# Attention scores with the keys on the partitions: one change to a two-layer hybrid block

## The chip, the cores and the metric

The kernel runs on one core of a Trainium2 chip. A core has a matrix engine (TensorE, PE in the profile; its weight loads are PEld), a vector engine (VectorE, DVE), ScalarE (ACT), GpSimd (POOL) and a queue for transfers (SyncE, SP). Each executes its own instructions in program order and waits for the others by semaphores. The metric is the device time of one execution in microseconds; lower is better.

## The reference, cut to what matters

Two layers of a block over 1024 latent tokens and 256 context tokens, width 1024. Each layer normalizes and modulates, multiplies by one input projection, and splits its columns among a bidirectional gated DeltaNet (a recurrence over chunks of tokens), a latent attention with four heads, and a short convolution. All are gated, concatenated and sent through one output projection. Only the attention is touched here:

```python
def mla_queries(q_a, norm_g, w_qb, cos, sin):
    q = (rmsnorm(q_a, norm_g) @ w_qb).reshape(bn, t, B_HEADS, B_NOPE + B_ROPE)   # 4 heads x (64 + 32)
    if cos is not None:
        q = jnp.concatenate([q[..., :B_NOPE], rope_2d(q[..., B_NOPE:], cos, sin)], axis=-1)
    return q
...
        s = jnp.einsum("bqhd,bkhd->bhqk", q_blk, k).astype(F32) * scale
        p = jax.nn.softmax(s, axis=-1).astype(v.dtype)
        return jnp.einsum("bhqk,bkhd->bqhd", p, v)
...
    b_x = softmax_attention(q_x, jnp.concatenate([k_x, k_c], axis=1),
                            jnp.concatenate([v_x, v_c], axis=1)) * jax.nn.silu(xz_b)
```

Latent queries read all 1280 keys, context queries (first layer only) the 256 context keys. All data are float32.

## The kernel before

Tokens are cut into ten tiles of 128: 0 to 7 are latent, 8 and 9 context. `GROUPS` joins them to pieces of 512, 512 and 256 tokens. A layer is a chain of stages: gate and convolution blocks with the large input projection (L447), preparation of the recurrence's chunks, and then a stage in which the attention and the recurrence run side by side, and at whose end the output projection starts. That stage is where the change lies.

Products that need nearly full precision are made from three passes of a high and a low part (`mm3`, L83): high by high, low by high, high by low. A low part is the value less its high part, which is one DVE instruction, after an ACT copy that rounds to the high part. Products of probabilities and values, of the recurrence, and transposes by the identity matrix are plain float32.

The attention of one layer, before. `k_pair` (L1013 to L1026) makes the keys of two heads, 64 channels from the compressed keys and 32 rotary ones, in `kh` and `kl` (latent, high and low) and `kc` (context). `v_tile` makes the values of a token tile. `q_tile` makes the queries of one token tile: two transposes (L827, L828), six passes of 384 columns with the queries as the stationary operand, the rotation on POOL (L345 to L350), four transposes (L844), and the split into high and low parts (L848). The unit of work is a query tile and a head, 40 in the first layer and 32 in the second:

- `a_scores` (L1031): 128 queries on the partitions, keys as moving columns in pieces of 512, 512 and 256, three passes each; DVE takes the row maximum of each piece (L1041) and of the three (L1045); ACT takes the exponential with the negated maximum as the bias and sums the row as it goes (L1048).
- `a_trans` (L1053): ten transposes of the probabilities (L1058), copied out by ACT and DVE (L1060).
- `a_pv` (L1065): probabilities by values, 64 output channels of one head in one half of the array's columns and of the other head in the other half (`tile_position`, L1074).
- `a_out` (L1085): the reciprocal row sums are transposed, spread over the partitions by a small matmul (L1095), and multiplied with the result and the gate.

The recurrence, `recur` (L1107 to L1189), one generator for each direction, has four kinds of products per tile and direction (L1144, L1154, L1164, L1169 and L1170) and vector instructions between them (L1146, L1156, L1173, L1181; L1150 on POOL).

What sets the order: a small planner, `Sched` (L85), holds generators as lanes with a due time. The attention loop (L1302) writes its instructions directly and calls `sch.tick(dt)` with a guessed duration; each tick advances the planner's clock and lets the lanes that are due issue their next piece. The instruction order of each engine that comes out of this is rearranged once more by the framework's scheduler when the kernel is built, so the order of the code is only roughly that of the engines.

Of the kernel before, what the change touches and what calls it, by code (L numbers as in the profile page):

```python
# [14 lines left out]
KD = 8  # L15
NT = 10
# [5 lines left out]
C_ID, C_SUM, C_UP, C_LO, C_ONE, C_COS, C_SIN, C_SEL, C_END = 0, 128, 160, 288, 416, 544, 672, 800, 1056  # L22
# [6 lines left out]
def kernel(  # L29
# [16 lines left out]
    cst_in: bass.AP,  # L46
    out: bass.AP,
# [95 lines left out]
    bx_d = dram([128, NT, 2, 128], "bx_d")  # L143
# [142 lines left out]
    # the first modulation  # L286
# [28 lines left out]
    for l in range(DEPTH):  # L315
# [4 lines left out]
        # token-layout block  # L320
# [52 lines left out]
        # gates  # L373
# [50 lines left out]
        # channel-layout blocks  # L424
# [126 lines left out]
        # z and short-conv blocks  # L551
# [53 lines left out]
        # chunk preparation  # L605
# [170 lines left out]
        # weights and keys of the latent attention  # L776
# [3 lines left out]
        def load_qkv():  # L780
            wq_r = st([128, 2, 384], "P4", name="wq_r")
            S.dma_start(out=wq_r[:, 0], in_=mla_w_qb[l, 0:128, :])
            S.dma_start(out=wq_r[0:64, 1], in_=mla_w_qb[l, 128:192, :])
# [4 lines left out]
            wq = st([128, 2, 2, 384], "W8", F32R, name="wq")  # L788
            for b_, m in ((0, 128), (1, 64)):
                V.tensor_scalar(wq_r[0:m, b_], wq_r[0:m, b_], col[0:m, 75 + b_:76 + b_], sc, ALU.mult, ALU.mult)  # L790
                split(wq_r[0:m, b_], wq[0:m, 0, b_], wq[0:m, 1, b_])
# [4 lines left out]
            sch.add(q_tile(act[0]))  # L796
# [3 lines left out]
        def kv_lane(i):  # L800
            while len(merged) < NT:
                yield 1.0
            if "c" not in qkv:
                qkv["c"] = [st([128, TOK], "T5", F32R, name=f"ckv{w}") for w in range(2)]
                qkv["pe"] = st([128, TOK], "T5", name="pes")
            ckv, pes = qkv["c"], qkv["pe"]
# [13 lines left out]
        Q = {}  # L820

        def q_tile(i):
            mq = st([128, 192], "P2", name="mq")
            S.dma_start(out=mq, in_=mla_d[i, :, 0:192])
            yield 3.0
            pt = bank()
            T.transpose(pt[:, 0:128], mq[:, 0:128], ident)  # L827
            T.transpose(pt[0:64, 128:256], mq[:, 128:192], ident)  # L828
            qa = st([128, 2, 2, 128], "P2", F32R, name="qa")
            for b_, m in ((0, 128), (1, 64)):  # L830
                src = pt[0:m, b_ * 128:b_ * 128 + 128]
                copy_a(qa[0:m, 0, b_], src)
                V.tensor_tensor(out=qa[0:m, 1, b_], in0=src, in1=qa[0:m, 0, b_].bitcast(F32), op=ALU.subtract)
            yield 2.0
            pq = bank()
            mm3(pq[:, 0:384], [(qa[0:m, a_, b_], qkv["wq"][0:m, w_, b_]) for b_, m in ((0, 128), (1, 64)) for a_, w_ in ((0, 0), (1, 0), (0, 1))])
            qs = st([128, 4, 96], "P2", name="qs")
            copy_a(qs.rearrange("p h f -> p (h f)"), pq[:, 0:384])
            if i < NX:
                rope(qs[:, :, 64:96], i, 4)  # L840
            yield 6.0
            pt = bank()
            for h in range(4):
                T.transpose(pt[0:96, h * 128:(h + 1) * 128], qs[:, h, :], ident)  # L844
            qt = st([128, 2, 4, 128], "P4", F32R, name="qt")
            p3 = pt[0:96].rearrange("p (h f) -> p h f", h=4)
            copy_a(qt[0:96, 0], p3)
            V.tensor_tensor(out=qt[0:96, 1], in0=p3, in1=qt[0:96, 0].bitcast(F32), op=ALU.subtract)  # L848
            Q[i] = dict(qt=qt, sums=st([128, 4, 3], "st", name="sums"), P={}, PT={}, o={})

        # the start of a layer: two gate blocks beside the rows of h that are still being made
# [148 lines left out]
        # latent attention  # L1000
# [3 lines left out]
        vx = st([128, NT, 256], "B16", name="vx")  # L1004
# [7 lines left out]
        def k_pair(h0):  # L1012
            ws = wk[:, :, 64 * h0:64 * h0 + 128]  # L1013
            for g in (2, 0, 1):
# [4 lines left out]
                for r in range(2):  # L1019
# [5 lines left out]
                    copy_a(hi[64:96], pes[64:96, cs])  # L1025
                    (V if h < 2 else P).tensor_tensor(out=lo[64:96], in0=pes[64:96, cs], in1=hi[64:96].bitcast(F32), op=ALU.subtract)  # L1026

        def a_parts(i):
            return [(g, t0, n) for g, (t0, n) in enumerate(GROUPS) if i < NX or g == 2]

        def a_scores(i, h):  # L1031
            q = Q[i]
            qt = q["qt"]
            pr = a_parts(i)
            mx = st([128, 4], "st", name="mx")
            banks = []
            for g, t0, n in pr:
                pb = bank()
                kk = (kh[0:96, h, t0:t0 + n], kl[0:96, h, t0:t0 + n]) if g < 2 else (kc[0:96, 0, h, :], kc[0:96, 1, h, :])
                mm3(pb[:, 0:n], ((qt[0:96, 0, h], kk[0]), (qt[0:96, 1, h], kk[0]), (qt[0:96, 0, h], kk[1])))  # L1040
                V.tensor_reduce(mx[:, g:g + 1], pb[:, 0:n], AX.X, ALU.max)  # L1041
                banks.append(pb)
            g0 = pr[0][0]
            nm = st([128, 1], "st", name="nm")
            V.tensor_reduce(nm, mx[:, g0:3], AX.X, ALU.max, negate=True)  # L1045
            p = st([128, TOK], "T5", name="prob")
            for (g, t0, n), pb in zip(pr, banks):
                A.activation(out=p[:, t0:t0 + n], in_=pb[:, 0:n], func=ACTF.Exp, bias=nm, scale=1.0, accum_out=q["sums"][:, h, g:g + 1])  # L1048
            q["P"][h] = p
# [366 lines left out]
```

## Time and profile before

| quantity | value |
|---|---|
| median of three runs | 1771.2 us (1770.02 to 1771.27) |
| profiled execution, first to last instruction | 1772.6 us |
| mean granted TensorE clock | 0.984 of full speed |
| busy PE / DVE / ACT / POOL | 97% / 62% / 48% / 26% |
| attention stage of the first layer | 552.7 to 833.1 us |
| attention stage of the second layer | 1408.0 to 1672.5 us |
| PE busy in those two | 532.65 of 544.90 us |

The profile gives for each group of instructions its busy time and the mean duration of one. On PE neighbouring matmuls overlap, so the mean duration is longer than what one adds; the distance from one start to the next tells that. A float32 matmul leaves two records, so that counts of records are twice the number of matmuls there (L1074: 1312 records, 656 matmuls).

### The profile page before, as it was taken

The page shows a single profiled execution, that of the slowest core. Times are in us where ns is not written, and L with a number is a line of the kernel's source. Part 1 is how long each engine was busy: PE and PEld are TensorE (multiplying, and loading weights), DVE is VectorE, ACT ScalarE, POOL GpSimd, SP SyncE. Part 2 cuts the span into 40 slices and gives each one's busy share as a digit, 9 for nine tenths or more (in the row PEclk, how much of TensorE's full clock was granted, in tenths as well). Part 3 has the DMA queues.
Part 4 walks back from the last instruction along what each step waited for, and adds up shares of the span by engine and source line. Part 5 has one row for each costly group of instructions (what it writes and reads, how often), then busy time and mean ns, then how long its engine had stood idle before and what let it go on. Part 6 is the DMA issues. An engine that isn't in the chain of part 4 may idle for free.

```text
span 1772.6 us, 33569 instructions
## 1 busy us (share of the span) xinstructions
PE 1717.4 (97%) x12644; PEld 1430.9 (81%) x12644; DVE 1101.7 (62%) x2178; ACT 842.7 (48%) x2287; POOL 467.5 (26%) x779
## 2 busy tenths in 40 slices
PE   7999999999999999999999999998999899999998
PEld 5787887788878989888887987786787689997786
DVE  3435668787634676656566156599885476675564
ACT  4644663223536444665345346551334655445631
POOL 1410435222211212322230302562113211123221
PEclk8999999999999999999999999998999899999999
DMA  9333556563335866323343224556434535553541
GB/s 365 123 109 100 178 169 188 178 202 101 100 123 184 278 200 196 103 69 127 124 125 129 81 71 133 181 166 212 138 116 123 183 122 181 163 180 113 161 131 48
DMA packets 194770, 264.74 MB, mean 149 GB/s; under 512 B 48304, under 2 KB 116912, under 8 KB 194608
## 3 DMA queue, kind: packets, MB, share of 16 engines
q1 hardware_dynamic: 194608, 262.59, 45.9%
q8 instruction: 100, 1.64, 0.4%
q14 instruction: 62, 0.51, 0.1%
HBM read 183.17 MB, written 79.36 MB: 148 GB/s over the span
## 4 chain that ended last, share of the span: by engine, by line
PE 83%; DVE 6%; DMA 5%; ACT 3%; issue 2%; POOL 1%; SPq 1%; POOLq 0%; DVEq 0%; ACTq 0%
PE bank L447 33%; PE bank L83 23%; PE bank L1074 5%; PE bank L1058 5%; PE bank L1154 2%; PE bank L1144 2%; PE bank L1164 2%; PE bank L1170 2%; PE bank L1169 2%; DMA wa<-in_w_ada_dram 1%; PE bank L511 1%; PE bank L187 1%; DVE pr L675 1%; DVE Mb L676 1%; DMA gcb<-row_d 1%
## 5 line engine op out<-in xcount | busy, mean ns | idle before, releaser
L447 PE MATMUL bank<-h_hi,w 128*128 128x512 f32 x1664 | 433.2, 403 | 2.4 <-DVE h_hi L282 2.4
L447 PEld LDWEIGHTS bank<-h_hi,w 128*128 128x128 f32 x1664 | 305.2, 189 | 75.2 <-issue 4.8
L447 PE MATMUL bank<-h_lo,w 128*128 128x512 f32 x832 | 217.5, 402 | 0.0
L447 PEld LDWEIGHTS bank<-h_lo,w 128*128 128x128 f32 x832 | 154.2, 189 | 37.3 <-issue 1.6
L461 DVE SCALAR_TENSOR_TENSOR acc<-pad,col,acc 128x1284 f32<-128x1284 f32 (+1 forms) x104 | 158.0, 1520 | 8.5 <-ACT acc L458 6.8
L83 PE MATMUL bank<-wo_hi,mix 128*128 128x512 f32 x576 | 141.7, 398 | 0.0
L1048 ACT ACTIVATE prob<-bank,nm 128x512 f32<-128x512 f32 (+1 forms) x200 | 119.4, 607 | 28.3 <-DVE nm L1045 28.1
L1041 DVE TENSOR_REDUCE mx<-bank 128x1 f32<-128x512 f32 (+1 forms) x200 | 112.5, 591 | 23.4 <-PE bank L83 22.6
L83 PEld LDWEIGHTS bank<-wo_hi,mix 128*128 128x128 f32 x576 | 106.9, 188 | 24.8
L75 DVE TENSOR_TENSOR w<-wr,w 128x1024 fp32r<-128x1024 f32 x52 | 66.0, 1271 | 85.1 <-ACT w L74 84.8
L447 PE MATMUL bank<-h_c,w 128*128 128x256 f32 x816 | 110.1, 287 | 0.0
L447 PEld LDWEIGHTS bank<-h_c,w 128*128 128x128 f32 x816 | 102.5, 190 | 6.6 <-issue 4.5
L1150 POOL TENSOR_TENSOR ring<-ring,qx 128x512 f32<-128x512 f32 x32 | 40.7, 1272 | 215.6 <-DMA ring<-row_d 126.9
L1058 PE MATMUL bank<-cst,prob 128*128 128x128 f32 x656 | 94.9, 282 | 2.8 <-ACT prob L1048 2.5
L1074 PE MATMUL bank<-probT,vx 128*64 128x128 f32 x1312 | 97.4, 280 | 0.0
L74 ACT ACTIVATE w<-wr 128x1024 fp32r<-128x1024 f32 x52 | 54.9, 1060 | 73.7 <-PE bank L447 54.7
L1074 PEld LDWEIGHTS bank<-probT,vx 128*64 128x64 f32 x1312 | 78.5, 139 | 12.8 <-issue 7.8
L1060 DVE COPY probT<-bank 128x512 f32<-128x512 f32 x64 | 44.3, 692 | 68.1 <-PE bank L1058 65.5
L83 PE MATMUL bank<-kh,qt 96*128 96x512 f32 x256 | 86.1, 417 | 0.5 <-DVE kl L1024 0.4
L1058 PEld LDWEIGHTS bank<-cst,prob 128*128 128x128 f32 x656 | 71.8, 142 | 18.1 <-issue 11.2
L78 ACT ACTIVATE probT<-bank 128x256 f32<-128x256 f32 (+1 forms) x136 | 61.9, 488 | 35.4 <-PE bank L1058 35.3
L676 DVE TENSOR_TENSOR Mb<-Mb,pr 128x31 f32<-128x31 f32 (+15 forms) x186 | 70.4, 378 | 5.0
(298 smaller groups left out, 3329.8 us busy)
## 6 DMA issues: line engine op xcount, KB each, us to landing
wr<-in_w_blk_dram SPq DMA_DIRECT2D x52, 512.0 KB
wa<-in_w_ada_dram SPq DMA_DIRECT2D x32, 512.0 KB
gcb<-row_d SPq DMA_DIRECT2D x20, 512.0 KB
nn_d<-N SPq DMA_DIRECT2D x20, 512.0 KB
ring<-vr_d SPq DMA_DIRECT2D x40, 256.0 KB
ring<-nn_d SPq DMA_DIRECT2D x40, 256.0 KB
ring<-kt_d SPq DMA_DIRECT2D x40, 256.0 KB
qk_d<-gcb SPq DMA_DIRECT2D x18, 512.0 KB
```

Of the source, the lines that this page charges most:

```text
L74: A.activation(out=hi, in_=raw, func=ACTF.Copy)
L75: eng.tensor_tensor(out=lo, in0=raw, in1=hi.bitcast(F32), op=ALU.subtract)
L78: A.activation(out=out, in_=in_, func=ACTF.Copy)
L83: T.matmul(outp, lhsT=lh, rhs=rh, start=q == 0, stop=q == n - 1)
L447: T.matmul(pb[:, 0:n], lhsT=self.w[:, wi, k, :], rhs=hg[g][hi][:, k, :], start=q + k == 0, stop=q == 2 and k == KD - 1)
L461: V.scalar_tensor_tensor(out=acc[:, 2:hi], in0=pad[:, 2 + t - r:hi + t - r], scalar=col[:, ci:ci + 1], in1=acc[:, 2:hi], op0=ALU.mult, op1 ...
L676: V.tensor_tensor(out=N[:, 0:k, k:32], in0=N[:, 0:k, k:32], in1=pv, op=ALU.subtract)
L1041: V.tensor_reduce(mx[:, g:g + 1], pb[:, 0:n], AX.X, ALU.max)
L1048: A.activation(out=p[:, t0:t0 + n], in_=pb[:, 0:n], func=ACTF.Exp, bias=nm, scale=1.0, accum_out=q["sums"][:, h, g:g + 1])
L1058: T.transpose(pT[:, k * 128:(k + 1) * 128], p[:, t0 + k * 128:t0 + (k + 1) * 128], ident)
L1060: V.tensor_copy(out=pb[:, t0:t0 + n], in_=pT[:, 0:n])
L1074: T.matmul(o3[64 * r:64 * r + 64, pair, :], lhsT=vx[:, kt, hh * 64:hh * 64 + 64], rhs=q["PT"][hh][:, kt * 128:(kt + 1) * 128], start=kt == ...
```

## The change

Scores are made the other way round, for a group of queries and a pair of heads at a time: 128 keys on the partitions (the stationary operand), up to 512 queries as moving columns. The probabilities come out with the keys on the partitions, as the product with the values wants them, and that product is 512 columns wide. There are six such units in the first layer and four in the second.

A maximum per query cannot be a bias any more, since the queries now lie along the columns. It is found by a separate pass, `a_max` (queries on the partitions, high parts only, for one query tile and head), one unit ahead; `a_shift` transposes the negated maxima to row 96 of the queries' tile, and the keys have a row of ones there, so that the first of the three passes has 97 rows of contraction and subtracts the maximum. Before the first unit, `warm` issues all eight maxima of it; in the first layer the two small context units are warmed, and the eight maxima of the third unit are issued within the second one's only step.

The row sums are taken by adding the probabilities over key tiles, head 0 of the pair on DVE (L1122) and head 1 on POOL (L1120), and at the end a product with ones (L1132) adds over the partitions; a reciprocal of 128x512 (L1135) follows. The queries are made in channel layout, 512 tokens at a time: `q_rows` transposes the rows of a group (L846, L847), `q_head` makes a head with five passes of 512 columns (the last two stack high and low part of the 64 remaining rows) and rotates with extra weight columns and a table `rot` (L871, L872 on DVE, one sum on POOL). The weights of the output projection are loaded in tiles of 512 columns, and the attention's result goes to memory as [2, 128, tokens].

```diff
-        def a_scores(i, h):
...
-                mm3(pb[:, 0:n], ((qt[0:96, 0, h], kk[0]), (qt[0:96, 1, h], kk[0]), (qt[0:96, 0, h], kk[1])))
-                V.tensor_reduce(mx[:, g:g + 1], pb[:, 0:n], AX.X, ALU.max)
...
-                A.activation(out=p[:, t0:t0 + n], in_=pb[:, 0:n], func=ACTF.Exp, bias=nm, scale=1.0, accum_out=q["sums"][:, h, g:g + 1])
+        def a_max(g, h, j):
...
+                T.matmul(pb[:, 0:n], lhsT=q["qt"][0:96, 0, j * 128:(j + 1) * 128],
+                         rhs=kh[0:96, h, t0:t0 + n] if gk < 2 else kc[0:96, 0, h, :], start=True, stop=True)
+                V.tensor_reduce(mx[:, gk:gk + 1], pb[:, 0:n], AX.X, ALU.max)
+            V.tensor_reduce(q["nm"][:, j:j + 1], mx[:, 2 if g == 2 else 0:3], AX.X, ALU.max, negate=True)
+        def a_shift(g, h):
...
+                T.transpose(pn[0:1, j * 128:(j + 1) * 128], q["nm"][:, j:j + 1], ident)
+            copy_a(q["qt"][96:97, 0, 0:n], pn[0:1, 0:n])
+        def a_scores(u, kts):
...
+            for kk, kt in enumerate(kts):
+                for r in range(2):
...
+                    mm3(pb, [(hi[0:97], qt[0:97, 0, 0:n]), (hi[0:96], qt[0:96, 1, 0:n]), (lo[0:96], qt[0:96, 0, 0:n])])
+                    A.activation(out=pts[r][:, kk, 0:n], in_=pb, func=ACTF.Exp)
+                sch.tick(0.0028 * n)
-        def a_trans(i, h):
...
+        def a_pv(u, kts, pts):
...
+                    T.matmul(u["po"][64 * r:64 * r + 64, 0:n], lhsT=vx[:, kt, hh * 64:hh * 64 + 64], rhs=pts[r][:, kk, 0:n],
+                             start=kt == keys[0], stop=kt == keys[-1], tile_position=(0, 64 * r))
...
+                    if r:
+                        P.tensor_tensor(acc, a0, a1, ALU.add)
+                    else:
+                        V.tensor_tensor(out=acc, in0=a0, in1=a1, op=ALU.add)
+        def a_out(u):
...
+                T.matmul(sm[64 * r:64 * r + 64], lhsT=cst[:, C_ONE:C_ONE + 64], rhs=vt[:, 5 + r, 0:n], start=True, stop=True,
+                         tile_position=(0, 64 * r))
+            V.reciprocal(out=rc, in_=sm)
+            V.tensor_tensor(out=rc, in0=u["po"][:, 0:n], in1=rc, op=ALU.mult)
+            P.tensor_tensor(zb, zb, rc, ALU.mult)
...
+        def q_head(g, h):
...
+            mm3(pq, [(wq[:, 0, h], qa[:, 0, 0:n]), (wq[:, 0, h], qa[:, 1, 0:n]), (wq[:, 1, h], qa[:, 0, 0:n]),
+                     (wq[:, 2, h], qb[:, 0:n]), (wq[:, 3, h], qb[:, 0:n])])
...
+            V.tensor_tensor(out=lo[0:w], in0=pq[0:w], in1=hi[0:w].bitcast(F32), op=ALU.subtract)
+                V.tensor_tensor(out=r1[64:96], in0=pq[64:96], in1=rot[64:96], op=ALU.mult)
+                V.tensor_tensor(out=r2[64:96], in0=pq[96:128], in1=rot[96:128], op=ALU.mult)
...
+        def warm(u, vs):
+            for g, h in heads(u):
+                q_head(g, h)
+            sch.tick(2.4)
+            mg = maxes(u)
+            for i in vs:
+                next(mg, None)
+                v_tile(i)
+                sch.tick(0.9)
...
+            for q, kts in enumerate(steps):
+                pts = a_scores(u, kts)
+                if prev:
+                    a_pv(*prev)
...
+                    many = 8 if len(steps) == 1 else (0, 2, 3, 3, 0)[q]
+                    for _ in range(many):
+                        next(mg)
+                        sch.tick(0.6)
+                    if q == len(steps) - 1:
+                        for gh in heads(nxt):
+                            a_shift(*gh)
```

Below, what this does to the order of the engines at three places. In the changed kernel the lines of the recurrence stand 40 lower (L1144 is L1184, L1154 is L1194, L1164 is L1204) and `mm3` is L84.

First PE, before, in the second layer's attention: transposes of queries (L844) and of probabilities (L1058), recurrence, and PV (L1074, on `probT` and `vx`).

```order
L1164 MATMUL bank<-vd,ring_14513 128x128 x8
L1144 MATMUL bank<-ring_14513,kx 128x128 x5
L844 MATMUL bank<-cst,qs 96x128 x4
L1074 MATMUL bank<-probT,vx 64x128 x9
L1144 MATMUL bank<-ring_14513,kx 128x128 x2
L1074 MATMUL bank<-probT,vx 64x128
L1144 MATMUL bank<-ring_14513,kx 128x128
L1074 MATMUL bank<-probT,vx 64x128 x10
L1058 MATMUL bank<-cst,prob 128x128 x10
L1154 MATMUL bank<-ring_14513,ring_14512 128x128 x4
```

And PE in the changed kernel in the middle of the first layer's attention, where PV is L1109 (on `probT` and `vt`), the pass for the maxima L1072.

```order
L1109 MATMUL bank<-probT,vt 64x512
L1194 MATMUL bank<-ring_5654 128x128 x4
L1072 MATMUL bank<-kh,qt 128x512 x2
L1072 MATMUL bank<-kc,qt 128x256
L1109 MATMUL bank<-probT,vt 64x512
L1072 MATMUL bank<-kh,qt 128x512
L1109 MATMUL bank<-probT,vt 64x512
L1072 MATMUL bank<-kh,qt 128x512
L1109 MATMUL bank<-probT,vt 64x512
L1072 MATMUL bank<-kc,qt 128x256
```

Before, the 20 matmuls of a PV are cut into runs of nine, one and ten by recurrence products; now single ones, one head's each, stand between recurrence products and passes for the maxima.

Next DVE in the changed kernel, first layer, second context unit: L867, L871 and L872 belong to `q_head`, L1074 and L1075 are the maxima, L1213 the recurrence.

```order
L867 TENSOR_TENSOR qt<-bank,qt 64x512
L871 TENSOR_TENSOR r_6163<-bank,rot 32x512
L872 TENSOR_TENSOR r_6164<-bank,rot 32x512
L867 TENSOR_TENSOR qt<-bank,qt 64x512
L871 TENSOR_TENSOR r_6180<-bank,rot 32x512
L872 TENSOR_TENSOR r_6181<-bank,rot 32x512
L1074 TENSOR_REDUCE mx<-bank 128x1 x3
L1075 TENSOR_REDUCE nm<-mx 128x1
L1213 SCALAR_TENSOR_TENSOR ring_5654<-ring_5654,gtot,bank 128x128 x8
L1074 TENSOR_REDUCE mx<-bank 128x1 x3
L1075 TENSOR_REDUCE nm<-mx 128x1
L1074 TENSOR_REDUCE mx<-bank 128x1 x9
```

All 24 reductions of the third unit's maxima stand in one stretch here; before, three reductions followed each unit's scores.

Then PE in the changed kernel at the same place: the last maxima, the transposes that carry them to row 96 (L1082), and the first scores of the unit.

```order
L1072 MATMUL bank<-kh,qt 128x512 x2
L1072 MATMUL bank<-kc,qt 128x256
L1072 MATMUL bank<-kh,qt 128x512 x2
L1072 MATMUL bank<-kc,qt 128x256
L1082 MATMUL bank<-cst,nm 1x128 x8
L84 MATMUL bank<-qt,kh 128x512 x2
L84 MATMUL bank<-qt,kl 128x512
```

Before, no transpose of this kind existed, and the scores of a unit waited for its queries and keys alone; the maxima of a unit now stand ahead of its first score on PE.

## Rows read from the trace of the kernel before

**Rows 1.** the page's chain that ended last, by engine: shares of the span

```profile
PE 83%; DVE 6%; DMA 5%; ACT 3%; issue 2%; POOL 1%; SPq 1%; POOLq 0%; DVEq 0%; ACTq 0%
```

**Rows 2.** windows of the first stretches; last line: sum over both attention stages

```profile
552.70:621.00 68.30, 64.32 (x496) 58.69 (x495) 47.15 (x122) 37.41 (x111) 13.96 (x16) 0.98 0.84 279
...
1408.00:1446.00 38.00, 34.80 (x228) 30.50 (x228) 31.61 (x66) 24.07 (x64) 9.44 (x12) 0.91 0.49 168
...
sum 544.90, PE 532.65 PEld 469.33 DVE 364.45 ACT 310.55 POOL 126.75; mean PE 88.77 PEld 78.22 DVE 60.74 ACT 51.76 POOL 21.12
```

**Rows 3.** timeline of PE in two stretches: start, duration, line, tile, count

```profile
646.42 0.43 PE L1074 MATMUL bank<-probT,vx 128*64 128x128 f32 x2
646.79 0.49 PE L1144 MATMUL bank<-ring,kx 128*128 128x128 f32 x2
647.21 0.44 PE L1074 MATMUL bank<-probT,vx 128*64 128x128 f32 x4
647.57 0.49 PE L1144 MATMUL bank<-ring,kx 128*128 128x128 f32 x2
...
650.10 1.31 PE L1058 MATMUL bank<-cst,prob 128*128 128x128 f32 x10
651.25 1.95 PE L1154 MATMUL bank<-ring 128*128 128x128 f32 x16
652.96 0.71 PE L83 MATMUL bank<-kh,qt 96*128 96x512 f32 x2
653.51 0.39 PE L83 MATMUL bank<-kl,qt 96*128 96x512 f32 x1
653.74 0.63 PE L83 MATMUL bank<-kh,qt 96*128 96x512 f32 x2
...
654.43 0.52 PE L83 MATMUL bank<-kc,qt 96*128 96x256 f32 x3
654.79 1.04 PE L1058 MATMUL bank<-cst,prob 128*128 128x128 f32 x8
...
1507.52 1.41 PE L83 MATMUL bank<-wq,qa 128*128 128x384 f32 x6
1508.87 1.09 PE L1058 MATMUL bank<-cst,prob 128*128 128x128 f32 x8
```

**Rows 4.** costliest groups of PE, shapes apart: count, busy, mean, idle

```profile
L1095 PE MATMUL bank<-r,cst 4*128 4x128 f32 x72 | 12.7, 296 | 0.0
```

**Rows 5.** groups of DVE, shapes apart: count, busy us, mean ns, idle

```profile
L1041 DVE TENSOR_REDUCE mx<-bank 128x1 f32<-128x512 f32 x128 | 87.6, 690 | 18.0 <-PE bank L83 17.3
...
L1060 DVE COPY probT<-bank 128x512 f32<-128x512 f32 x64 | 44.3, 692 | 68.1 <-PE bank L1058 65.5 <-DMA o_d<-ot 2.1
L1146 DVE SCALAR_TENSOR_TENSOR ring<-bank,negeg,ring 128x128 f32<-128x128 f32 x144 | 39.9, 344 | 12.4 <-PE bank L1144 11.1 <-DMA ring<-kt_d 0.8 <-DMA ring<-nn_d 0.5
...
L1041 DVE TENSOR_REDUCE mx<-bank 128x1 f32<-128x256 f32 x72 | 29.9, 416 | 5.3 <-PE bank L83 5.3
...
L613 DVE TENSOR_TENSOR gcb<-gcb 128x512 f32<-128x512 f32 x20 | 16.6, 829 | 24.1 <-POOL gcb L612 22.3 <-POOL pad L453 1.8
...
L848 DVE TENSOR_TENSOR qt<-bank,qt 96x512 fp32r<-96x512 f32 x18 | 12.3, 685 | 12.3 <-ACT qt L78 12.3
...
L1045 DVE TENSOR_REDUCE nm<-mx 128x1 f32<-128x3 f32 x64 | 9.9, 155 | 1.9
...
L384 DVE RECIPROCAL beta<-beta 128x80 f32<-128x80 f32 x2 | 1.3, 653 | 0.0
...
L529 DVE RECIPROCAL r<-r 128x40 f32<-128x40 f32 x2 | 0.8, 404 | 0.1
```

**Rows 6.** timeline of DVE at the start of layer 1's attention

```profile
1408.59 3.58 DVE L1026 TENSOR_TENSOR kl<-pes,kh 32x512 fp32r<-32x512 f32 x4
1412.10 2.38 DVE L1026 TENSOR_TENSOR kc<-pes,kc 32x256 fp32r<-32x256 f32 x2
```

**Rows 7.** groups of POOL, shapes apart

```profile
L1150 POOL TENSOR_TENSOR ring<-ring,qx 128x512 f32<-128x512 f32 x32 | 40.7, 1272 | 215.6 <-DMA ring<-row_d 126.9 <-PE bank L83 39.7 <-PE bank L1154 14.9
```

More of the change, by code (lines that the diff above doesn't have):

```diff
@@ L795, in load_qkv @@
             qkv.update(wq=wq, wk=wk)
[L796 removed]
+            sch.add(q_rows(qgs[0]))
         kvf = Flags()
@@ L1072, in a_pv @@
+        def a_pv(u, kts, pts):
+            g, pair = u["g"], u["pair"]
+            n = GROUPS[g][1]
+            keys = a_keys(g)
+            if "po" not in u:
+                u["po"] = bank()
+            for kk, kt in enumerate(kts):
                 for r in range(2):
                     hh = 2 * pair + r
-                    T.matmul(o3[64 * r:64 * r + 64, pair, :], lhsT=vx[:, kt, hh * 64:hh * 64 + 64],
-                             rhs=q["PT"][hh][:, kt * 128:(kt + 1) * 128], start=kt == kts[0], stop=kt == kts[-1],
-                             tile_position=(0, 64 * r))
@@ L1323 @@
-        sch.until(lambda: wof.ok(0) and not Q)
+        prev = None
+        for x_, u in enumerate(units):
+            g = u["g"]
+            keys = a_keys(g)
+            steps = [keys[q:q + 2] for q in range(0, len(keys), 2)]
+            warmed = 1 if last else 2
+            nxt = units[x_ + 1] if warmed <= x_ + 1 < nu else None
+            mg = maxes(nxt) if nxt else None
+            for q, kts in enumerate(steps):
+                pts = a_scores(u, kts)
+                if prev:
+                    a_pv(*prev)
+                    if prev[0] is not u:
+                        sch.add(a_out(prev[0]))
+                        for gh in heads(prev[0]):
+                            Q.pop(gh)
+                    sch.tick(0.0035 * GROUPS[prev[0]["g"]][1])
+                prev = (u, kts, pts)
+                if nxt:
+                    if q == 0:
+                        sch.until(lambda: nxt["g"] in QA)
+                        for gh in heads(nxt):
+                            q_head(*gh)
+                        sch.tick(2.4)
+                        if nxt["pair"] == 1 and nxt["g"] == 0:
+                            sch.add(q_rows(1))
+                    many = 8 if len(steps) == 1 else (0, 2, 3, 3, 0)[q]
+                    for _ in range(many):
+                        next(mg)
+                        sch.tick(0.6)
+                    if q == len(steps) - 1:
+                        for gh in heads(nxt):
+                            a_shift(*gh)
+                if x_ == nu - 1 and q in (1, 3):
+                    sch.until(lambda: len(recurred) == 2)
+                    ahead(q // 2)
@@ L1324 @@
+        a_pv(*prev)
+        sch.add(a_out(prev[0]))
+        Q.clear()
+        ahead(2)
+        sch.tick(1.8)
+        sch.until(lambda: wof.ok(0))
         for q in range(3, n_act + 3):
```

265 lines of the change are left out of this document (130 added, 135 removed).

## Prediction

> **What bounds the kernel now.** Read the chain of waits first [rows 1]: of the chain that ended last, TensorE (PE) carries 83% and VectorE (DVE) 6%. A change therefore pays what it takes from PE's instruction stream, and costs whatever it makes PE wait for. The table of windows [rows 2] narrows this to the stretches that are changed: the two attention stages last 544.9 us together and PE is busy in 532.7 of them, 12.2 idle. The idle time is partly in the layers' first stretches, 4.0 us (68.3 less 64.3) and 3.2 (38.0 less 34.8); DVE is busy 67% of all of it. So there are two accounts: PE's work, and PE's idle time where DVE is late. The profiled span, 1772.6 us, is 1.4 above the median of the runs, 1771.2. All terms are differences within that execution, and I add them to 1771.2.
>
> **Rates of PE.** PE runs in program order, so the time from one row's start to the next start is what the row costs [rows 3]. A pass of 512 columns: 0.23 us (653.51 to 653.74), of 256: 0.12 (654.43 to 654.79 for three). Transposes: 1.15 us for ten, 0.115 each. A recurrence product of 128x128 writes two records: 1.71 us for 16, 0.214 each. The product of probabilities and values (PV) fills half the columns, and its two heads stand in different halves. One matmul between others takes 0.37 us (646.42 to 646.79); a pair of them takes 0.36 (647.21 to 647.57). So what counts is the slot, pair or lone. At 128 columns I put it at 0.22 (a recurrence product has the same two records and takes 0.214), which leaves 0.15 for entering and leaving the half-column form.
>
> The Trainium skill says the same from its side: "TensorEngine Tiling (Array Packing)", Key Properties, has it that tiles work independently of each other but that a change of the tiling mode drains the engine. The 0.37 against 0.36 agrees; by that rule alone the drains below would be the only cost of breaking pairs up, and the empty half of the array is the rest of it.
>
> **PE's work, both layers.**
> - Scores: 64 full units of 6 passes of 512 and 3 of 256, and 8 context units, were 384 x 0.23 + 216 x 0.12 = 114.2. Turned round they are 480 x 0.23 + 24 x 0.12 = 113.3. Change -0.9. The extra contraction row rides along.
> - The 656 transposes of the probabilities go: 656 x 0.115 = -75.4. Instead 72 transposes carry the maxima into the queries' row 96: +8.3.
> - The separate pass for the maxima is one high-part product where scores have three: 128 x 0.23 + 72 x 0.12 = +38.0.
> - PV is the term that works against the change. Before, 656 matmuls stand in 78 runs on PE (36 of them a lone one), 362 slots: 362 x 0.22 + 78 x 0.15 = 91.3. After, 168 matmuls, four times as wide, stand in 96 runs, 64 of them a lone one because the order puts a recurrence product or a maximum between the two heads; that makes 114 slots of 512 and 5 of 256: 114 x 0.88 + 5 x 0.44 + 96 x 0.15 = 116.9. Change +25.6.
> - Queries: 108 passes at 0.225 (six in 1.35 us) and 108 transposes were 36.7; 80 passes of 512, 20 of 256 and 36 transposes are 24.9. Change -11.8.
> - Normalizing: the spreading of the reciprocals was 12.7 busy [rows 4]; 20 half-column products with ones, in pairs, are 8 x 0.88 + 2 x 0.44 = 7.9. Change -5.
> The sum is -21 us. Where PV's rate is wrong, it is by the slots: were every pair left together, there would be 84 slots and the term would fall by about 30.
>
> **DVE at the start of a layer.** The new order needs all eight maxima of a unit (two heads, four query tiles) before the unit's first score, since the shift is a row of the queries. Their cost [rows 5]: 16 reductions of 512 at 0.69, 8 of 256 at 0.42, 8 small ones at 0.155 = 15.6 us of DVE for 4.7 us of PE. In steady state the next unit's maxima lie beside this unit's scores. At two places they do not.
> - Layer 0, second context unit: its only step issues the eight maxima of the first 512-wide unit in one go. The DVE rows there (most of them shown under the change) are 1.4 (query splits), 4.1 (two heads: low part and two rotations, 0.69 each), 2.6 (a sum, the reciprocal, a product), 15.6, and 16 ring updates at 0.28 = 4.4: 28 us. The reciprocal of 256 columns comes from the two rows of 40 and 80 elements, 404 and 653 ns, hence 6.2 ns an element: 1.75 us. PE's rows of the same stretch are 2.3 + 0.4 + 4.7 + 32 recurrence products (6.8) + 0.9 = 15. PE then waits at the transposes of the maxima for 13 us, and everything queued behind them waits too.
> - Layer 1, first unit: DVE has the low parts of the rotary keys (3.58 and 2.38, [rows 6]), six key parts of 512 and three of 256 (5.4), 4.1 for two heads of queries, 15.6, then 3.5 and 2.2 of the recurrence: 36.7 us. PE has 10 query passes, the keys (3.5), eight value tiles (2.9), the maxima 4.7 and 6.8 of the recurrence: 20.2. It waits 16.5.
> That is 29.5 where 7.2 of idle stood. If DVE begins ahead of PE at these places as much as 10 us of it hides, and if what PE waits for now in layer 0 stays, nothing of the 7.2 goes: +12 to +27. I take +23.
>
> **Steady state.** Per 512-wide unit DVE has 15.6 for maxima, 9 sums at 0.83, 4.8 for queries, and a reciprocal of 512 (3.3) with its product (0.7): 31.9. The same work before (eight head and query tiles with two maxima of 512, one of 256, a small one and a copy of 0.69, 2.65 in all, and some 0.4 each for queries) was 24. With eight such units in 545 us DVE goes from 67% to 79%. The bounds are -5 (all of PE's idle time outside the starts goes) and +28 (each of seven units waits 4.0 for its last maximum, as the first stretch of layer 0 does now). I take +6, nearer the lower end since PE has 63 us of rows per unit to wait in.
> ScalarE gets lighter (the accumulator reads and most copies go) and hides. GpSimd gets 72 sums at 1.27 [rows 7], 92 us over 545, and is not full; nothing reads them until the unit's end.
>
> Sum: -21 + 23 + 6 = +8, so 1779 us.
>
> **Rivals.**
> 1. Faster: the starts hide. DVE is given its maxima early enough that the starts cost +5, and steady state costs nothing: -16, 1755. For it: the pass of the maxima needs only the high parts, which ScalarE makes, and PE has independent recurrence products there. Against it: DVE runs in program order too, and the low parts stand ahead of the maxima. If the lone PV matmuls also find their partner, another 20 go: 1735.
> 2. Slower, by one mechanism: the sums collide. The sums of one head run on DVE and of the other on GpSimd at the same time, 72 each, all three operands in the chip's working memory. The DVE sums of that kind take 829 ns [rows 5] where those that read a bank take 685, and if each of them is held for a whole GpSimd sum, 1.27, DVE gets 72 x 1.27 = 91 more, 11 a unit, and reaches 100% of the stage. From there on every further microsecond is PE's: about +30, 1801. Against it: only a collision at the start of each sum holds one.
> The Trainium skill states this one: "SBUF — State Buffer", Who interferes with whom, says that a DVE instruction with two SBUF inputs contends with a GpSimd instruction that reads SBUF, and the first to come holds the port for its whole length. No row here shows a hold of that length; 829 against 685 is the only sign.
> 3. No change: PE's -21 is eaten by the starts alone and steady state is free: 1771 to 1774.
>
> **How the numbers follow.** The forecast has a chance of 0.46, rival 1 0.28, rival 2 0.14, rival 3 0.12. About 0.2% (3.5 us) is what can be told from no change here. The forecast's own range is 1775 to 1792; the whole range takes in the upper part of rival 1 and rival 2: 1750 to 1802. Faster 0.29 (rival 1, and a little of the forecast's lower tail), same 0.13, slower 0.58.
>
> **What would show it.** The trace of the changed kernel should have PE idle for about 13 us ahead of the transposes of the maxima in layer 0, released by the negated maximum, and about 16 us at the same line early in layer 1; DVE there without a gap. PV should take some 117 us by starts, with lone matmuls about 1.03 us each. DVE should be near 80% of the stages. The forecast is wrong if DVE has idle time in those two stretches, if a lone 512-wide PV costs well under 0.9, or if the sums on DVE take over 1.5 us.

## The result and the profile after

The changed kernel takes 1792.7 us (median of four runs, 1788.3 to 1794.0) where the kernel before takes 1771.2 in the same comparison: +21.5 us, a ratio of 1.011 with a 95% interval of 1.008 to 1.014. The forecast was 1779 (1750 to 1802), slower: the direction is right, the size is a bit over a third of what came.

The profiled execution is 19.0 us longer (1791.6 against 1772.6). All of it lies in the two attention stages, which now take 564.8 us where they took 544.9 [rows 2]: 18.2 us more in the first layer (280.4 to 298.6) and 1.7 in the second (264.5 to 266.2). The windows of the changed kernel, with the columns of [rows 2]; the last line is the sum over both stages:

```profile
600.00:630.00 30.00, 19.44 (x101) 14.08 (x100) 24.38 (x57) 3.90 (x7) 8.41 (x8) 0.80 0.29 93
...
1425.40:1450.00 24.60, 18.60 (x84) 15.97 (x85) 23.15 (x38) 10.27 (x23) 10.40 (x8) 0.77 0.47 153
1450.00:1480.00 30.00, 26.35 (x147) 22.38 (x146) 22.57 (x57) 14.37 (x26) 7.53 (x6) 0.89 0.30 98
...
sum 564.80, PE 533.97 PEld 372.69 DVE 409.35 ACT 226.50 POOL 245.16; mean PE 44.50 PEld 31.06 DVE 34.11 ACT 18.87 POOL 20.43
```

Read the last line first. PE's busy time is 534.0 us, and it was 532.7: the 656 transposes are gone, and nothing is saved in the sum. The difference is PE's idle time, 30.8 us where it was 12.2. The other three lines are the places that the prediction named, the third unit of layer 0 and the first unit of layer 1: 10.6, 6.0 and 3.7 us idle, with DVE busy 24.4 of 30.0 and 23.2 of 24.6 us. The third number from the end is the granted clock: 0.80, 0.77 and 0.89, so part of these stretches ran at the lower level, 1.2 GHz. The two sums below are over all stretches of the two stages with a granted clock of 0.50 or 0.51, six in the changed kernel and then four in the kernel before:

```profile
sum 42.30, PE 33.34 PEld 28.38 DVE 26.52 ACT 14.65 POOL 13.04; mean PE 5.56 PEld 4.73 DVE 4.42 ACT 2.44 POOL 2.17
```

```profile
sum 13.60, PE 13.41 PEld 12.57 DVE 5.97 ACT 11.42 POOL 2.10; mean PE 3.35 PEld 3.14 DVE 1.49 ACT 2.85 POOL 0.52
```

PE works 33.3 us at the lower level where it worked 13.4. If all of the 20 us more would take half as long at the full level, they hold up to 10 us; that is an estimate from these two sums, and an upper bound.

The groups on PE that answer to [rows 4] and to the rates of [rows 3], shapes apart (count, busy us, mean ns, idle before):

```profile
L1109 PE MATMUL bank<-probT,vt 128*64 128x512 f32 x320 | 118.6, 611 | 1.1 <-ACT probT L1096 1.1
...
L1072 PE MATMUL bank<-kh,qt 96*128 96x512 f32 x128 | 50.2, 454 | 13.4 <-ACT qt L79 11.8 <-DVE ring L1186 1.3 <-ACT vt L79 0.2
...
L1072 PE MATMUL bank<-kc,qt 96*128 96x256 f32 x72 | 23.0, 324 | 1.1 <-ACT kc L79 0.8 <-DVE mx L1074 0.3
...
L1082 PE MATMUL bank<-cst,nm 128*1 128x128 f32 x72 | 12.0, 287 | 3.7 <-DVE nm L1075 3.7
```

Of the idle time, 11.8 us stand ahead of the pass for the maxima and are released by ScalarE's copy of the queries; only 3.7 are released by a negated maximum. PE's longest waits at the third unit, from 600 to 630 us (in total, times, longest):

```profile
PE bank L1072 <- ACT qt L79: 4.5, 1, 4.5
PE bank L1082 <- DVE nm L1075: 2.1, 1, 2.1
PE bank L84 <- DVE qb L853: 1.8, 1, 1.8
PE bank L1072 <- DVE ring L1186: 1.3, 2, 0.7
```

On DVE and POOL, answering to [rows 5, 7]:

```profile
L1074 DVE TENSOR_REDUCE mx<-bank 128x1 f32<-128x512 f32 x128 | 83.2, 684 | 8.9 <-PE bank L1072 8.1
L1122 DVE TENSOR_TENSOR vt<-vt,probT 128x512 f32<-128x512 f32 x64 | 68.3, 1068 | 18.7 <-ACT probT L1096 17.6
...
L1135 DVE RECIPROCAL vt<-bank 128x512 f32<-128x512 f32 x8 | 26.8, 3354 | 5.2 <-PE bank L1132 5.2
```

```profile
L1120 POOL TENSOR_TENSOR vt<-vt,probT 128x512 f32<-128x512 f32 x64 | 91.0, 1422 | 48.3 <-ACT probT L1096 45.7
```

The reciprocal is the 3.3 us that were worked out from 40 and 80 elements; the sums take 1.07 us in the mean, where 0.83 were reckoned. Both are means of two kinds. Here are two sums on DVE with the sum on POOL beside each (start, duration), and last the sums of the kernel before that gave the 0.83 (L613 in [rows 5]; shortest/median/longest in ns):

```profile
813.66 0.69 DVE L1122 TENSOR_TENSOR vt<-vt,probT 128x512 f32<-128x512 f32 x1 [0.32 <-ACT probT L1096]
813.70 1.78 POOL L1120 TENSOR_TENSOR vt<-vt,probT 128x512 f32<-128x512 f32 x1
...
1550.23 1.28 POOL L1120 TENSOR_TENSOR vt<-vt,probT 128x512 f32<-128x512 f32 x1
1550.28 1.78 DVE L1122 TENSOR_TENSOR vt<-vt,probT 128x512 f32<-128x512 f32 x1
```

```profile
L613 DVE TENSOR_TENSOR gcb<-gcb x20: 676/693/2372, 194.0 to 1192.5; 128x512 f32<-128x512 f32 x20
```

The one that starts second waits for the other's end: the DVE sum of 1550.28 ends 0.55 us behind POOL's, which ends at 1551.51. Of the 72 sums of this size on DVE, 43 start while POOL is at work and end 0.56 us in the mean after POOL's instruction does; the other 29 take 0.68 to 0.69. The 43 are 24.7 us longer together than at 0.69 each.

How PV looks on PE, in the timeline of the changed kernel (start, duration, line, tile, records; take the distances between starts):

```profile
723.34 0.50 PE L1072 MATMUL bank<-kh,qt 96*128 96x512 f32 x1
723.77 1.08 PE L1109 MATMUL bank<-probT,vt 128*64 128x512 f32 x4
724.78 0.49 PE L1072 MATMUL bank<-kh,qt 96*128 96x512 f32 x1
725.21 1.08 PE L1109 MATMUL bank<-probT,vt 128*64 128x512 f32 x4
726.21 0.39 PE L1072 MATMUL bank<-kc,qt 96*128 96x256 f32 x1
...
755.70 1.07 PE L1109 MATMUL bank<-probT,vt 128*64 128x512 f32 x2
756.70 0.49 PE L1184 MATMUL bank<-ring,kx 128*128 128x128 f32 x2
```

Four records are two matmuls, one for each head: 1.00 us (725.21 to 726.21). Two records are a lone one: 1.00 us too (755.70 to 756.70). The slot counts, as forecast. The pass for the maxima, set between PV matmuls, takes 0.43 us for 512 columns (724.78 to 725.21), where it was reckoned at 0.23.

### The profile page after: what moved, and what is told of

Its sections match the earlier page's. It is cut to its first block, busy times and chain, and to the rows that moved or that the text cites. A ratio compares the mean times of both kernels' runs of the same rounds, so it can differ in the third digit from the quotient of the medians.

```text
span 1791.6 us, 30054 instructions
## 1 busy us (share of the span) xinstructions
PE 1720.9 (96%) x11058; PEld 1336.6 (75%) x11058; DVE 1159.8 (65%) x2144; ACT 766.1 (43%) x1895; POOL 609.5 (34%) x811
## 4 chain that ended last, share of the span: by engine, by line
PE 53%; DVE 5%; ACT 2%; issue 2%; DMA 2%; POOL 1%; SPq 0%; POOLq 0%; DVEq 0%; ACTq 0%
PE bank L84 20%; PE bank L448 13%; PE bank L1109 6%; PE bank L1072 2%; PE bank L1204 2%; PE bank L1194 2%; PE bank L1210 2%; PE bank L1209 2%; PE bank L1184 1%; DVE mx L1074 1%; DVE pr L676 1%; DVE Mb L677 1%; PE bank L512 1%; PE bank L1132 1%; DMA mb_d<-dg 1%
## 5 line engine op out<-in xcount | busy, mean ns | idle before, releaser
L1096 ACT ACTIVATE probT<-bank 128x512 f32<-128x512 f32 (+1 forms) x168 | 96.4, 590 | 129.0 <-PE bank L84 123.8
L84 PE MATMUL bank<-wo_hi,mix 128*128 128x512 f32 x576 | 142.8, 398 | 0.0
L84 PEld LDWEIGHTS bank<-wo_hi,mix 128*128 128x128 f32 x576 | 106.8, 188 | 25.5 <-issue 0.8
L1109 PE MATMUL bank<-probT,vt 128*64 128x512 f32 (+1 forms) x336 | 121.4, 601 | 1.1 <-ACT probT L1096 1.1
L1074 DVE TENSOR_REDUCE mx<-bank 128x1 f32<-128x512 f32 (+1 forms) x200 | 106.8, 588 | 12.8 <-PE bank L1072 11.9
L1120 POOL TENSOR_TENSOR vt<-vt,probT 128x512 f32<-128x512 f32 x64 | 91.0, 1422 | 48.3 <-ACT probT L1096 45.7
L84 PE MATMUL bank<-qt,kh 97*128 97x512 f32 (+1 forms) x256 | 86.3, 419 | 3.3 <-ACT qt L79 3.2
L1122 DVE TENSOR_TENSOR vt<-vt,probT 128x512 f32<-128x512 f32 x64 | 68.3, 1068 | 18.7 <-ACT probT L1096 17.6
L1213 DVE SCALAR_TENSOR_TENSOR ring<-ring,gtot,bank 128x128 f32<-128x128 f32 x144 | 47.3, 345 | 42.6 <-PE bank L1209 33.6
L84 PE MATMUL bank<-wo_lo,mix 128*128 128x512 f32 x288 | 73.9, 395 | 0.0
L676 DVE TENSOR_TENSOR pr<-L,Mb 128x31 f32<-128x31 f32 (+15 forms) x186 | 68.5, 368 | 4.5
```

The lines of the kernel that those rows point to most:

```text
L84: T.matmul(outp, lhsT=lh, rhs=rh, start=q == 0, stop=q == n - 1)
L676: V.tensor_tensor(out=pv, in0=bc(L[:, 0:k, k], w), in1=N[:, k:k + 1, k:32].to_broadcast([128, k, w]), op=ALU.mult)
L1074: V.tensor_reduce(mx[:, gk:gk + 1], pb[:, 0:n], AX.X, ALU.max)
L1096: A.activation(out=pts[r][:, kk, 0:n], in_=pb, func=ACTF.Exp)
L1109: T.matmul(u["po"][64 * r:64 * r + 64, 0:n], lhsT=vx[:, kt, hh * 64:hh * 64 + 64], rhs=pts[r][:, kk, 0:n], start=kt == keys[0], stop=kt == ...
L1120: P.tensor_tensor(acc, a0, a1, ALU.add)
```

## The experiments

Twelve kernels ran, each compared with the kernel before on the same chip; the ratio to that kernel is what can be compared between them, and the changed kernel's is 1.011. The changed kernel's own interval is 1.008 to 1.014, so a difference from it of less than some 7 us is not told with certainty. Single executions of the kernels with pinned PV spread by about 1%, so stages of two such profiles are not compared below some 7 us either.

**e1, PV pinned.** `a_pv`:

```diff
-                    T.matmul(u["po"][64 * r:64 * r + 64, 0:n], ...)
+                    tc.keep_in_program_order(T.matmul(u["po"][64 * r:64 * r + 64, 0:n], ...))
```

> Only the order is changed: every PV matmul is pinned behind what stands before it in the code, so that the two heads' matmuls of a key tile stand side by side on PE (40 runs of four instead of 96 runs, 64 of them lone; 85 slots instead of 119). Theory A (a slot costs the same, pair or lone): PV's 114.5 us of starts fall by 34 x 0.88, about 30, and some 8 more for 53 fewer changes of form: 1755 to 1765. Theory B (the lone matmuls only filled time in which PE would wait for the exponentials or DVE anyway): PV falls as much, but PE's idle time grows by about the same: 1785 to 1795.

Measured: 1774.7 us, ratio 1.001 (0.999 to 1.003), half-way between the two theories. The sum over both stages, the PV group, and PE's longest waits in the first and in the second layer (in total, times, longest):

```profile
sum 546.50, PE 498.32 PEld 368.24 DVE 412.71 ACT 226.06 POOL 250.72; mean PE 41.53 PEld 30.69 DVE 34.39 ACT 18.84 POOL 20.89
```

```profile
L1109 PE MATMUL bank<-probT,vt 128*64 128x512 f32 x320 | 79.1, 616 | 0.0
```

```profile
PE bank L1072 <- ACT qt L79: 5.6, 2, 4.5
PE bank L1072 <- DVE mx L1074: 5.2, 3, 3.0
PE bank L84 <- ACT qt L79: 3.9, 5, 1.8
```

```profile
PE bank L84 <- ACT qt L79: 7.1, 5, 2.3
```

PV is busy 39.5 us less (118.6 to 79.1), and PE's busy time falls by 35.7; its idle time grows from 30.8 to 48.2. So keeping the pairs together takes back some 17.5 of the 21.5 us, and about half of what the lone slots cost PE had filled time in which PE has nothing else ready: waits for the shift and for the pass's banks come out from behind them.

**e2, no sums.** In `a_pv`, `ins = [(acc, ab_[0]), (acc, ab_[1])]` becomes `ins = []`, and the exponential gets `scale=0.01`.

> Leaves out the row sums of all but the first two key tiles of a unit, on DVE and on GpSimd (64 instructions on each are gone, 68 and 91 us), and scales the exponent so that nothing overflows; the values are not the reference's. If the sums collide and hold DVE (rival 2), DVE's load falls from 72% to 60% of the attention stages and the time by 15 us or more: 1775 or less. If what counts is where DVE has its maxima at the start of a layer, there are hardly any sums there, and steady state has slack: 1787 to 1794.

Measured: 1782.7 us, ratio 1.007 (1.004 to 1.009).

```profile
sum 559.20, PE 531.44 PEld 372.42 DVE 352.19 ACT 227.95 POOL 152.93; mean PE 265.72 PEld 186.21 DVE 176.09 ACT 113.98 POOL 76.46
```

DVE is 57 us lighter and POOL 92, and the time falls by about 7 us (1.011 to 1.007, intervals that overlap), less than rival 2's 15 and a little more than the other side allowed. The sums cost at most a part of the loss.

**e3, no reductions, and e4, no pass.** `a_max`:

```diff
                 T.matmul(pb[:, 0:n], lhsT=q["qt"][0:96, 0, ...], rhs=..., start=True, stop=True)   # e4: gone too
-                V.tensor_reduce(mx[:, gk:gk + 1], pb[:, 0:n], AX.X, ALU.max)
-            V.tensor_reduce(q["nm"][:, j:j + 1], ..., AX.X, ALU.max, negate=True)
```

Both also scale the exponent by 0.01 and fill the negated maxima with zeros instead.

> Leaves out the reductions of the maxima on DVE (200 and 72 instructions, 124 us), with the pass on PE and the transposes of a constant kept and the exponent scaled so that nothing overflows; the values are not the reference's. Theory A (DVE is late at the starts, PE waits there and then runs at half its clock for some us): PE's idle time of 30.9 us in the two stages falls to about the 12 of before, and the mean granted clock in the first 80 us of each stage goes back up: 19 + 8 less, 1762 to 1770. Rival (the maxima cost by their PE pass and by broken-up PV alone): 1785 to 1793.

> As e3, and leaves out the pass on PE too (200 matmuls, 54.2 us of starts, of which 38 at the full clock). Theory A: another 38 to 42 us less than e3, 1722 to 1732. Rival (the pass fills time in which PE would wait): less than 25 below e3.

Measured: e3 1757.2 us, ratio 0.992 (0.990 to 0.994); e4 1706.2, ratio 0.963 (0.961 to 0.966). The sums over both stages, e3 first (with the window that is shown of the changed kernel):

```profile
600.00:630.00 30.00, 23.51 (x143) 19.72 (x142) 13.33 (x28) 8.92 (x20) 8.96 (x8) 0.89 0.35 114
...
sum 528.80, PE 509.28 PEld 365.31 DVE 304.75 ACT 225.56 POOL 246.16; mean PE 84.88 PEld 60.89 DVE 50.79 ACT 37.59 POOL 41.03
```

```profile
sum 480.00, PE 460.86 PEld 333.35 DVE 304.31 ACT 225.24 POOL 244.17; mean PE 230.43 PEld 166.67 DVE 152.16 ACT 112.62 POOL 122.08
```

Without the reductions the stages are 36 us shorter, more than expected: 11.3 of it is idle time (30.8 to 19.5), and 24.7 is PE's busy time, though PE has the same matmuls; PV and the pass sit differently in the order when DVE is lighter (PV 12 us less by starts), and the granted clock around the third unit is 0.89 instead of 0.80. The pass on PE is worth a further 51 us, against 38 by its columns. Both parts of the maxima cost time, the pass more than its columns, and both rivals fall.

**e5, less DVE at the starts.** `k_pair`:

```diff
-                    V.tensor_tensor(out=lo[0:64], in0=pr, in1=hi[0:64].bitcast(F32), op=ALU.subtract)
+                    if r == 0:
+                        V.tensor_tensor(out=lo[0:64], in0=pr, in1=hi[0:64].bitcast(F32), op=ALU.subtract)
+                    else:
...
+                        copy_a(rk[0:64, 0:n], pr)
+                        P.tensor_tensor(lo[0:64], rk[0:64, 0:n], hi[0:64].bitcast(F32), ALU.subtract)
...
-                    (V if h < 2 else P).tensor_tensor(out=lo[64:96], ...)
...
+                    if h == 0:
+                        P.tensor_tensor(lo[64:96], pes[64:96, cs], hi[64:96].bitcast(F32), ALU.subtract)
+                    else:
+                        copy_a(lo[64:96], lo0[64:96].bitcast(F32))
```

> Same computation, less DVE at the start of a layer: the low parts of the rotary keys are made once on GpSimd and copied to the other heads by ScalarE, and half the low parts of the other key channels are subtracted on GpSimd from a ScalarE copy. Of DVE's 36.7 us ahead of the first score of layer 1, 5.9 and about 2.5 go; the burst of the third unit in layer 0 keeps its 28. Theory A (DVE's total ahead of the first score is what PE waits for): 6 to 10 us less idle in layer 1, 3 to 6 in layer 0, and 2 to 4 of the slow clock: 1776 to 1784 where the changed kernel would be 1793. Rival (PE waits for single chains, query copy by ScalarE to rotation to copy, and not for DVE's total): 1788 to 1796.

Measured: 1790.0 us, ratio 1.009 (1.006 to 1.011): a miss. The wait ahead of the first pass of layer 1 is even longer:

```profile
PE bank L1081 <- ACT qt L79: 8.0, 2, 7.4
```

DVE had idle stretches there, 3.6 us ahead of PE's wait and then 1.5 and 1.6, each ended by a copy on ScalarE. What the changed kernel's PE waited for is seen in its timeline at that place, from the first head's query copy to the first pass for the maxima, all engines:

```profile
1430.52 0.59 ACT L79 ACTIVATE qt<-bank 64x512 fp32r<-64x512 f32 x1 [1.01 <-PE bank L84]
...
1431.48 0.40 PE L84 MATMUL bank<-ckv,wk 128*128 128x256 f32 x2
1431.48 0.94 DVE L1054 TENSOR_TENSOR kc<-pes,kc 32x256 fp32r<-32x256 f32 x1
1432.45 1.28 DVE L1052 TENSOR_TENSOR kl<-bank,kh 64x512 fp32r<-64x512 f32 x2
...
1433.66 0.67 DVE L867 TENSOR_TENSOR qt<-bank,qt 64x512 fp32r<-64x512 f32 x1
...
1434.36 0.69 DVE L871 TENSOR_TENSOR r<-bank,rot 32x512 f32<-32x512 f32 x1
...
1435.08 0.69 DVE L872 TENSOR_TENSOR r<-bank,rot 32x512 f32<-32x512 f32 x1
...
1435.91 1.25 POOL L873 TENSOR_TENSOR r<-r,r 32x512 f32<-32x512 f32 x1 [3.76 <-issue]
...
1437.19 0.62 ACT L79 ACTIVATE qt<-r 32x512 fp32r<-32x512 f32 x1 [1.93 <-POOL r L873]
...
1437.87 1.22 PE L1072 MATMUL bank<-kh,qt 96*128 96x512 f32 x2 [5.99 <-ACT qt L79]
...
1438.89 0.41 PE L1072 MATMUL bank<-kc,qt 96*128 96x256 f32 x1
```

The last 4.2 us are one query's chain: low part and two rotations on DVE, the sum on POOL, a copy on ScalarE, each starting as the one before ends. But the query was copied by 1431.11, and DVE took it up at 1433.66: until then DVE worked without a gap on low parts of the keys. So of PE's wait of 6.0 us some 2.5 are DVE's queue and 3.4 the chain. e5 shortened that queue and put copies on ScalarE in front of the same chain, so it does not part the two. The first pass behind the wait takes 0.51 us for 512 columns (1.02 for two), at a granted clock of 0.50.

**e6, e7, e8: e1 and e5 together, and two variations, each on top of the one before.** e7 changes `(0, 2, 3, 3, 0)[q]` to `(1, 3, 3, 1, 0)[q]` and moves the query's low part behind its rotation; e8 changes `if r:` at the sums to `if r or pair == 0:`.

> e1 and e5 together. If the two costs are independent, 18 and 10 less: 1762 to 1768. If the idle time that pairing uncovered in e1 (17 us) is at the same places, more is won: down to 1755.

> e6, with the maxima of the next unit spread as 1, 3, 3, 1, 0 over the five steps instead of 0, 2, 3, 3, 0, and the rotation of the queries ahead of their low part, so that the shift into row 96 is ready before the unit's first score. In e1 PE waited 11 us for ScalarE's copy of the shift, up to 2.3 at each unit. If that chain is late because the last maxima come late: 6 to 9 less than e6. If it is late because DVE has a queue: no change.

> e7, with the sums of both heads on GpSimd in every first pair of a group: 34 us less on DVE (of 413 in the stages), 45 us more on GpSimd. If DVE's load still holds PE in steady state: 3 to 8 less than e7. If GpSimd's own work at the end of a stage (splitting the output weights) is then late: 0 to 5 more.

Measured: e6 1781.0 us, ratio 1.004 (1.003 to 1.006); e7 1790.8, 1.010 (1.007 to 1.012); e8 1789.0, 1.008 (1.006 to 1.011). Three misses: what e5 moves makes e1 worse by 0.3% (intervals that overlap a little, on two chips), and e7's two changes, which no run parts, make it worse again by 0.5%; e8 can't be told from e7. Moving DVE's work about in these ways does not pay.

**e9, e10, e11: the chains themselves.** e9 is e1 with the shift ahead of PV, e10 adds the first unit's queries ahead of the keys, e11 the third unit's queries ahead of the context scores, with its eight maxima dealt four and four to the two context units (cut here):

```diff
                 pts = a_scores(u, kts)
+                if nxt and q == 4:                       # e9
+                    for gh in heads(nxt):
+                        a_shift(*gh)
...
-            sch.add(q_rows(qgs[0]))
+            sch.add(q_first())                           # e10: q_rows, then both q_head
...
-            warm(units[1], ())
-            sch.add(q_rows(0))
+            sch.add(q_rows(0))                           # e11
+            warm(units[1], ())
+            sch.until(lambda: 0 in QA)
+            for gh in heads(units[2]):
+                q_head(*gh)
```

> e1, with the shift into row 96 of the next unit issued right behind the last step's scores (ahead of that step's PV) instead of behind it, so that PE has PV to do while ScalarE copies the shift. In e1 PE waited 11 us for that copy (3.9 and 7.1). If the wait is the bare chain transposes, copy, score: 6 to 9 less than e1's 1774.7, 1766 to 1769. If the maxima themselves are late behind DVE's queue: within 3 of e1.

> e9, with the queries of a layer's first unit made as soon as their weights and rows are there, ahead of the keys, while PE still has the input projection. e5 took 8 us of DVE's work away there and won nothing, so the theory now is that PE waits for one chain (query product, ScalarE copy, two rotations on DVE, GpSimd sum, ScalarE copy), 6.0 us in layer 1. If so: that wait goes and some 2 us of slow clock behind it, 6 to 8 less than e9. If it is DVE's total after all: PE waits as long one step later, within 3 of e9.

> e10, with the third unit's queries of layer 0 made before the two context units' scores (the context queries of a pair share a tile, which frees the place) and its eight maxima dealt four and four to the two context units' steps. In e1 PE waits there 1.8 for the split of the queries, 4.5 for the same chain, and 3.5 for banks and the last maxima. If the chain is the cost: 5 to 8 less than e10, with the clock. If DVE's 28 us against PE's 15 is what binds the stretch: the same idle time, spread out, within 3 of e10.

Measured: e9 1775.8 us, ratio 1.0005 (0.9992 to 1.0019), no change from e1; e10 1772.1, 0.998 (0.996 to 0.999); e11 1774.1, 0.999 (0.996 to 1.001). The queries ahead of the keys are worth about 0.26%, 4.6 us (3.6 between the medians, and the two intervals just touch), less than the 6 to 8 expected; the other two chains give nothing that can be told. In e10 the wait for the queries early in layer 1, 5.1 us in e1, is gone, and one for the keys stands there:

```profile
PE bank L1079 <- ACT kh L79: 3.4, 2, 3.2
```

**e12, low parts on GpSimd.** In e11's `k_pair`, `(V if h < 2 else P).tensor_tensor(out=lo[64:96], ...)` becomes `P.tensor_tensor(lo[64:96], ...)`.

> e11, with the low parts of the rotary keys of all four heads on GpSimd (before: two heads on DVE). In e11 PE waits 4.0 and 1.5 us for ScalarE's copies of the context keys at the start of layer 0; these wait for DVE's reads of the same bank, which stand behind four such low parts (3.54 us). Unlike e5 nothing is added to ScalarE, which there had 4 us of copies ahead of the queries'. If that chain through DVE is the wait: 4 to 8 less than e11's 1774, 1766 to 1770, and clearly under before. If something else follows close behind it: within 3 of e11.

Measured: 1768.5 us, ratio 0.996 (0.9945 to 0.9976), a version that beats both kernels by a little.

```profile
sum 539.00, PE 501.10 PEld 372.59 DVE 405.85 ACT 222.65 POOL 256.48; mean PE 250.55 PEld 186.29 DVE 202.92 ACT 111.32 POOL 128.24
```

PE's busy time is 31.6 us less than before the change, and its idle time, 37.9, three times as much: much of the transposes' gain is there once PV is paired, and most of that is still given back in waits. (Some 5 us of the 31.6 are query passes that now stand ahead of the stage; over the whole execution, the slowest of e12's seven, PE is busy 1687.5 us where it was 1717.4.) The clock takes its share here too, by the stretches with 0.50 or 0.51 of e12's two stages:

```profile
sum 64.70, PE 55.82 PEld 44.60 DVE 40.17 ACT 23.41 POOL 36.21; mean PE 5.58 PEld 4.46 DVE 4.02 ACT 2.34 POOL 3.62
```

PE works 55.8 us at the lower level, against 13.4 in the kernel before.

## Why the prediction was right or wrong

The terms, against the same sums in the two profiles (for each PE instruction of the stages the time to the next start, less idle time):

| term, us | predicted | measured |
|---|---|---|
| scores | -0.9 | +1.9 |
| transposes of the probabilities | -75.4 | -80.8 |
| shift | +8.3 | +10.4 |
| pass for the maxima | +38.0 | +54.2 |
| PV | +25.6 | +22.6 |
| queries | -11.8 | -9.2 |
| normalizing | -5 | -2.1 |
| recurrence, keys, values | 0 | +4.3 |
| PE's work | -21 | +1.3 |
| PE's idle time | +29 | +18.6 |
| sum | +8 | +19.9 |

- **PV, right.** The term against the change was sized within 3 us, and its mechanism, a lone slot as dear as a pair, is shown by the 1.00 us of both and by e1, where 34 fewer slots took 39.5 us off the group's busy time. e1 also shows what the lone slots cost the time, some 18 us, since half of that work stood where PE would have waited.
- **The pass for the maxima, mis-sized by 16.** "One high-part product where scores have three: 128 x 0.23 + 72 x 0.12" takes the rate from long runs. Here 29 of the wide ones stand ahead of another kind of matmul and take 0.39 on average, 0.43 between PV matmuls (4.6 us more); 67 others at the full clock take 0.275 (2.9); 32 stand at the two starts (3.7, about half of it in the seven at a lower granted clock), and the narrow ones have 4.7 more. e4 shows the same from the other side: taking out matmuls of 38 us by columns saved 51.
- **The starts, right in place, too large, and wrong about the wait.** PE idles 10.6 us at the third unit (13 forecast) and 9.7 in layer 1's first 55 us (16.5 forecast). The step that failed is "PE then waits at the transposes of the maxima": 2.1 us stand there at the third unit, and none in layer 1. At the third unit 4.5 us are the wait for the queries' copy, and 5.7, those 2.1 among them, are ended in pieces by DVE instructions; in layer 1 the wait ahead of the pass is some 2.5 of DVE's queue and 3.4 of the query's chain. So DVE's queue costs PE about as much (8.2) as the chain does (7.9), but spread over the stretch and not as one wait at its end. "DVE there without a gap" holds in layer 1; at the third unit DVE has four gaps of 0.8 to 1.0 us. e5 took some 8 us of DVE away in layer 1 and won nothing, but lengthened the chain on ScalarE. e3, which took all the reductions, won 36 us, so DVE's work does cost, but through the order and the clock as much as through waiting. A slip in the sum besides: 29.5 less 7.2 is 22, not 23, and were all of the 7.2 to stay, the upper bound would be 29.5 and not 27.
- **The clock was left out.** The prediction had no term for what a wait does to the work behind it. The granted clock of these stretches is 0.77 to 0.89 where [rows 2] have 0.98 and 0.91, and two passes that should take 0.46 us take 1.02 right behind a wait. By the two sums over the stretches at the lower level, up to 10 of the 22 us that the work was short by are this, part of the pass's excess, of the scores' and of the recurrence's +3.1; no run parts it cleanly.
- **DVE's load and rival 2, the sums' collision.** DVE is busy 409.4 of 564.8 us, 72%, where 79 was forecast (the rival's 100 would by its own terms have been 96). The collision is there, and it is the one that the rival described; 829 ns was not a collision-free sum, since the median of those is 693. But it added 24.7 us to DVE and not 91, because 29 of the 72 sums meet no running GpSimd instruction and the others wait only for what is left of one. It costs the time little: e2, which took most of the sums away, won about 7 us, with intervals that overlap, where 30 was the price. The Trainium skill ("SBUF — State Buffer", Who interferes with whom) calls the port pair that DVE and GpSimd share an exclusive lock, with the order of issue deciding who blocks; the trace agrees, by the two sums of 1.78 us above.

Right for the wrong reasons in part, then: the forecast's two errors, 22 us too little work and 10 us too much waiting, went against each other. With the work as forecast and the waiting as it came the sum would have been -2, so even the direction owes something to luck.

Still open: what binds the starts once the queries are early. e9 to e12 took out one wait after another, and PE's idle time over the whole execution stayed between 83 and 91 us, as in e1 (91), where the changed kernel has 71 and the kernel before 55.

## What to carry to other kernels

Where a matmul fills half of the array's columns, count slots in the order that the scheduler made, not matmuls, and pin the two halves together before judging the layout. Take the rate of an added matmul from where it will stand: between other kinds, and behind waits, it cost 40% more than its columns. When work leaves the engine that bounds, look what it was covering: here paired PV took 36 us of work off PE, and 17 of them came back as waits.

## What the runs showed of the hardware

A 512-wide float32 matmul on half the columns takes 1.00 us between other kinds, alone or paired. A high-part pass of 512 columns between two such takes 0.43 us instead of 0.23. A reciprocal of 128x512 on DVE takes 3.35 us, 6.5 ns for each element of a row. A 128x512 sum on DVE takes 0.69 us with GpSimd free; one that starts while GpSimd is summing ends 0.56 us after GpSimd's instruction (up to 1.80 us in all), and a GpSimd sum that starts second takes up to 1.78 instead of 1.27.
